# A transformer layer on one core: query norm in two portions, modulation pieces re-timed, a scaling moved to VectorE

## The chip, the cores and the metric

The kernel runs on one core of a Trainium2 chip. The metric is the device time of one execution in microseconds (us). The kernel before takes 1704.09 us, the median of three runs (1702.79, 1704.09 and 1705.93 us).

The engines have the names of the profile: PE (TensorE, the matmuls), PEld (its weight loads), DVE (VectorE), ACT (ScalarE), POOL (GpSimd) and SP (SyncE, which here issues DMAs; its queue is SPq). Each engine works through its own queue in order.

## The reference

One layer of a diffusion backbone: 256 latent tokens `x` and 256 context tokens `ctx`, width 2048, everything in fp32. Cut to what matters:

```python
m_lat = adaln(c, w_ada, b_ada)      # silu(c) @ w_ada, six chunks: shift, scale, gate, shift2, scale2, gate2
m_ctx = adaln(c_ctx, w_ada, b_ada)
hc = modulate(rms_norm(ctx, norm1_g), m_ctx[0], m_ctx[1])
ka_c, va_c, kb_c, vb_c = split_kv(hc @ w_in[:, :KV_WIDTH], ...)      # keys are normalised
h = modulate(rms_norm(x, norm1_g), m_lat[0], m_lat[1])
ka, va, kb, vb = split_kv(...); qa, qb, ga, gb = split_qg(h @ w_in, ...)   # q = rms_norm(q)
qa, ka, qb, kb = apply_rope(...)
o_a = gqa(qa, [ka_c, ka], [va_c, va])            # 16 heads, 4 key heads
o_b = diff_attn(qb, [kb_c, kb], [vb_c, vb])      # 8 heads, two softmaxes, then rms_norm of o
merged = sigmoid(ga) * (o_a @ w_br_a) + sigmoid(gb) * (o_b @ w_br_b)
x = x + gate * (merged @ w_out)
x = x + gate2 * swiglu(modulate(rms_norm(x, norm2_g), shift2, scale2))
```

## The kernel before

**Products in three matmuls.** Each weight is split into a high and a low part in the matmul's type, and each product is three matmuls (`mm3`, L241 hi by hi, L242 hi by lo, L243 lo by hi). A weight tile is 128 x 1024 fp32, 512 KB: 256 rows of a group of 512 columns. `load_w` (L221) fetches it on SP's queue (L224) into the ring `wraw` of seven slots, ACT casts it to `whi` (L235), and DVE forms the difference `wlo` (L237). Both rings, `whi` and `wlo`, have three slots, so ACT and DVE can be no more than three weight tiles ahead of PE. With the two query tiles of 128 tokens a weight tile gives 12 matmuls of 128 x 512; in the key and value stage, with four token tiles, 24.

**Stages.** Start; keys and values, in steps of input rows (`kv_group`, two, four and eight and more k-tiles); query groups of 512 columns, gates and attention units side by side (`filler`, `project`, `front`, `back`: 16 units of branch b, then 16 of a); branch A's projection (loop ahead of L989); out-projection (L1075); norm; FFN.

**Modulation.** The shift and scale of the first norm come in pieces of 512 KB (`ada_cond`, L281 to L335) that PE multiplies by the conditioning vectors (L314). They are loaded either into a slot of the `wraw` ring (L294), into a large tile (L299), or, for the pieces n = 2 and 3 of a step of four k-tiles, in two halves into scratch buffers `nr` and `p` (L303). `modulated` makes the high and low input rows `xT` and `cT` from them (L356 to L360). The other modulation vectors (gate chunk 2, scale chunk 4, shift chunk 3, and gate2 in the FFN) are made by DVE: `ada_pieces` (L447) fetches a piece of 512 KB into the `wraw` ring and adds it, times one number of the conditioning vector, onto a row `ada` (L459), placed behind the newest `wlo`. `ada_later` gives out these pieces, and `take(later, n)` takes n of them. `side_work` (L868) takes one every second turn while queries of branch a are not all there, and two in three turns afterwards. What is left is taken in branch A's loop and by `drain(later)` (L989), and `ada_everywhere` (L990) then spreads the shift row over the partitions.

**Query norm and rotation.** `norm_rope` (L481) squares a tile of 128 x 512 on ACT (L490), reduces it on DVE (L492), makes the reciprocal root (`rstd_of`: DVE L123, then POOL's pow L124) and rotates: two products with the tables (L501, L503), a subtraction and an addition over halves (L505, L506), and the product with the reciprocal root (L507). `q_evac` (L743) calls it at once for the first token tile of a query group and, by `after(2)`, two pieces of the weight loop later for the second. `after(n, f)` runs f n pieces later. In a unit of branch b, `back` (L803) copies the output `on` to SBUF, makes its reciprocal root (`rstdo`) and scales `on` by it on ACT (L842).

**Order.** The Tile framework orders each engine's queue by its own scheduler. `tc.issue_after(ins)` puts an instruction behind another one in the queue.

Of the kernel before, what the change touches and what calls it, by code (L numbers as in the profile page):

```python
# [17 lines left out]
P = 128  # L18
# [28 lines left out]
def hybrid_block(ctx: ExitStack, tc: tile.TileContext, t: dict, out: bass.AP):  # L47
# [161 lines left out]
        nc.vector.tensor_scalar(out=neglam, in0=neglam, scalar1=-LAM_INIT, scalar2=None, op0=ALU.add)  # L209


    last_hi, last_lo = [], []

    def load_raw(r0, c0, n=2):
        raw = wp.tile([P, WK, CG], F32, tag="wraw", bufs=WRAW, name="wraw")
# [5 lines left out]

    def load_w(src, r0, c0, nk=WK, in_big=False):
        raw = wp.tile([P, WK, CG], F32, tag="wraw", bufs=WRAW, name="wraw")
        nc.sync.dma_start(out=raw[:, 0:nk], in_=src[r0:r0 + nk * P, c0:c0 + CG].rearrange("(k p) c -> p k c", p=P))  # L224
# [55 lines left out]
    def ada_cond(k0, nk):  # L280
# [4 lines left out]
        for part in range(2):  # L285
            aps = s_ps("ada")
            held = []
            for q in range(0, NKT, kk):
                piece = t["ada_t"][n0].rearrange("p (k c) -> p k c", c=ncol)
                n0 += 1  # L290
                n = q // kk
                if nk < 4 or n > 3:
                    wt = wp.tile([P, 2 * CG], F32, tag="wraw", bufs=WRAW, name="wada").rearrange("p (k c) -> p k c", c=ncol)
                    nc.sync.dma_start(out=wt, in_=piece)  # L294
                elif n < 2:
                    if n == 0:
                        two = big_tile("wada2").rearrange("p (n k c) -> p n k c", n=2, c=ncol)
                    wt = two[:, n]
                    nc.sync.dma_start(out=wt, in_=piece)  # L299
                else:  # L300
                    wt = [scratch("wada1", tag=tag, bufs=b) for tag, b in (("nr", 2), ("p", 4))]
                    for j in range(2):
                        nc.sync.dma_start(out=wt[j], in_=piece[:, j, :])  # L303
                held += [(q + j, wt[j] if nk == 4 and 1 < n < 4 else wt[:, j, :]) for j in range(kk)]
                last = q + kk == NKT
                if k0 and not last:
                    if nk == 4 and n == 3:
                        yield None
                    continue
                for k, rhs in held[::-1] if k0 else held:  # L310
                    g = k % 4
                    early, late_k = k < 4, k >= NKT - 4
                    with tc.issue_after(last_pe[0].ins) if k0 == 1 and k == held[-1][0] else nullcontext():
                        last_pe[0] = nc.tensor.matmul(aps[32 * g:32 * g + 32, 0:ncol], lhsT=cst[:, k, :], rhs=rhs,  # L314
                                                      start=late_k if k0 else early, stop=early if k0 else late_k)
# [168 lines left out]
    def norm_rope(src, br, qk, tok):  # L484
# [14 lines left out]
        else:  # L499
# [5 lines left out]
            nc.vector.tensor_tensor(out=o3[:, :, 0:half], in0=o3[:, :, 0:half], in1=b3[:, :, half:hd], op=ALU.subtract)  # L505
            nc.vector.tensor_tensor(out=o3[:, :, half:hd], in0=o3[:, :, half:hd], in1=b3[:, :, 0:half], op=ALU.add)  # L506
        nc.vector.tensor_tensor(out=o3, in0=o3, in1=r.unsqueeze(2).to_broadcast([P, nh, hd]), op=ALU.mult)  # L507
        return o


# [232 lines left out]
    def q_evac(qT, br):  # L743
# [58 lines left out]
    def back(br, u, pr):  # L802
# [39 lines left out]
        nc.scalar.mul(out=on, in_=on, mul=r)  # L842
# [101 lines left out]
    for cg in range(4):  # L944
# [35 lines left out]
        for k, _ in enumerate(project(w_bra, oT, AH, cg * CG, gated)):  # L980
# [201 lines left out]
```

## Time and profile before

| | before |
|---|---|
| median of three runs | 1704.09 us |
| the profiled execution's own time | 1703.83 us |
| its span, first to last instruction | 1701.7 us |
| PE busy, instructions | 1676.8 us (99%), 7889 |
| DVE busy | 1138.4 us (67%) |
| ACT busy | 779.0 us (46%) |
| mean DMA rate | 243 GB/s |
| mean granted PE clock | 0.997 |

Rows of the profile read so. A timeline row has the start in us, the duration in us, the engine, line, operation, output <- input, shapes, how many; and, in brackets, how long the engine was idle before it and what ended that. Matmuls overlap: at the full clock they start 0.23 us apart and each lasts 0.39. DVE rows overlap slightly too, so prices are taken start to start where rows follow one another. A row of windows has the stretch, its length, the busy time of PE, PEld, DVE, ACT and POOL with the number of instructions, the granted PE clock (1.00 is full), the busy share of the DMA engines and GB/s. A row of waits has the waiting engine and its line, what ended the wait, the sum in us, the number, and the longest.

### The profile page before, as it was taken

To read this page: it belongs to the slowest core of one execution; us is meant where nothing else is said; L and a number is where in the kernel's file an instruction comes from. 1 tells how busy PE (TensorE), PEld (TensorE's weight loads), DVE (VectorE), ACT (ScalarE), POOL (GpSimd) and SP (SyncE) were. 2 spreads that over 40 slices of the span, in tenths; PEclk is the share of its full clock that TensorE was granted. 3 is DMA by queue.
4 is the path that set the end of the run, shared out by engine and by line. 5 is a ranking of instruction groups with operands and counts; after the bars stand their busy time and mean duration, and the time that the engine had idled before them with its cause. 6 is when DMAs were issued, how large, how long until landed. Compare 5 with 4: busy or idle time off the path is not lost.

```text
span 1701.7 us, 21519 instructions
## 1 busy us (share of the span) xinstructions
PE 1676.8 (99%) x7889; PEld 1355.1 (80%) x7889; DVE 1138.4 (67%) x1438; ACT 779.0 (46%) x1071; POOL 209.3 (12%) x296
## 2 busy tenths in 40 slices
PE   7999999999999999999999999999999999999998
PEld 5677778887887778888888888888888888888887
DVE  5665779798687878996666755566666666554454
ACT  5221222246666656577544534444444444333332
POOL 0200002011231210011111101111111111100000
PEclk9999999999999999999999999999999999999999
DMA  9787875778766768776777857788888888766662
GB/s 352 288 316 275 304 253 157 234 252 256 246 180 216 222 225 272 246 238 212 256 265 237 294 175 221 235 263 267 263 272 263 269 274 253 238 218 195 216 207 88
DMA packets 181860, 413.08 MB, mean 243 GB/s; under 512 B 15065, under 2 KB 16298, under 8 KB 181498
## 3 DMA queue, kind: packets, MB, share of 16 engines
q1 hardware_dynamic: 169482, 374.17, 67.3%
q0 software_dynamic: 12272, 37.53, 7.4%
q8 instruction: 62, 1.02, 0.3%
q14 instruction: 44, 0.36, 0.1%
HBM read 395.35 MB, written 16.29 MB: 242 GB/s over the span
## 4 chain that ended last, share of the span: by engine, by line
PE 75%; issue 10%; DVE 6%; DMA 4%; POOL 3%; ACT 2%; SPq 0%; POOLq 0%; DVEq 0%; ACTq 0%
PE mm L241 22%; PE mm L242 22%; PE mm L243 22%; DVE wlo L237 2%; PE ada L314 1%; POOL fturn L1091 1%; ACT whi L235 1%; PE ptp L814 1%; DMA turn_d<-fpart 1%; DMA fturn<-turn_d 1%; DMA wraw<-in_w_in_dram 1%; DVE ada L459 1%; PE mm L401 1%; PE o L835 1%; DVE mx L736 1%
## 5 line engine op out<-in xcount | busy, mean ns | idle before, releaser
L237 DVE TENSOR_TENSOR wlo<-wraw,whi 128x1024 fp32r<-128x1024 f32 x498 | 606.8, 1220 | 443.9 <-ACT whi L235 442.9
L235 ACT CAST whi<-wraw 128x1024 fp32r<-128x1024 f32 x498 | 522.4, 1050 | 714.0 <-PE mm L243 607.2
L242 PE MATMUL mm<-wlo,hT 128*128 128x512 f32 x684 | 266.3, 389 | 0.1
L243 PE MATMUL mm<-whi,hT 128*128 128x512 f32 x684 | 266.1, 389 | 0.0
L241 PE MATMUL mm<-whi,hT 128*128 128x512 f32 x684 | 266.1, 389 | 0.0
L241 PE MATMUL mm<-whi,xT 128*128 128x512 f32 x630 | 252.7, 402 | 1.3 <-ACT xT L359 1.2
L242 PE MATMUL mm<-wlo,xT 128*128 128x512 f32 x630 | 247.0, 392 | 4.3 <-DVE wlo L237 4.3
L243 PE MATMUL mm<-whi,xT 128*128 128x512 f32 x630 | 246.9, 392 | 0.0
L459 DVE SCALAR_TENSOR_TENSOR ada<-wada,vt,ada 128x1024 f32<-128x1024 f32 x120 | 152.0, 1277 | 0.0
L242 PEld LDWEIGHTS mm<-wlo,hT 128*128 128x128 f32 x684 | 128.4, 188 | 27.7 <-DVE wlo L237 0.9
L241 PEld LDWEIGHTS mm<-whi,hT 128*128 128x128 f32 x684 | 128.4, 188 | 26.7
L243 PEld LDWEIGHTS mm<-whi,hT 128*128 128x128 f32 x684 | 128.4, 188 | 26.5
L241 PEld LDWEIGHTS mm<-whi,xT 128*128 128x128 f32 x630 | 118.6, 188 | 32.7 <-issue 7.0
L242 PEld LDWEIGHTS mm<-wlo,xT 128*128 128x128 f32 x630 | 118.8, 189 | 28.2 <-DVE wlo L237 5.7
L243 PEld LDWEIGHTS mm<-whi,xT 128*128 128x128 f32 x630 | 118.5, 188 | 26.0 <-DVE xT L360 0.3
L241 PE MATMUL mm<-whi,fT 128*128 128x512 f32 x354 | 137.5, 388 | 0.5 <-DVE y L1127 0.5
L242 PE MATMUL mm<-wlo,fT 128*128 128x512 f32 x354 | 137.3, 388 | 0.0
L243 PE MATMUL mm<-whi,fT 128*128 128x512 f32 x354 | 137.3, 388 | 0.0
L241 PEld LDWEIGHTS mm<-whi,fT 128*128 128x128 f32 x354 | 66.4, 188 | 15.0 <-issue 0.8
L243 PEld LDWEIGHTS mm<-whi,fT 128*128 128x128 f32 x354 | 66.5, 188 | 13.8
L242 PEld LDWEIGHTS mm<-wlo,fT 128*128 128x128 f32 x354 | 66.4, 188 | 13.7
L241 PE MATMUL mm<-whi,oT 128*128 128x512 f32 x192 | 75.9, 396 | 0.0
(236 smaller groups left out, 2150.4 us busy)
## 6 DMA issues: line engine op xcount, KB each, us to landing
wraw<-in_w_in_dram SPq DMA_DIRECT2D x159, 512.0 KB, 4.7
wada<-in_w_ada_dram SPq DMA_DIRECT2D x128, 512.0 KB, 4.6
wraw<-in_w_ff_gate_dram SPq DMA_DIRECT2D x88, 512.0 KB, 4.6
wraw<-in_w_ff_up_dram SPq DMA_DIRECT2D x88, 512.0 KB, 5.4
wraw<-in_w_ff_down_dram SPq DMA_DIRECT2D x88, 512.0 KB, 4.8
wada<-in_ada_t_dram SPq DMA_DIRECT2D x52, 512.0 KB, 7.8
wraw<-in_w_br_a_dram SPq DMA_DIRECT2D x32, 512.0 KB, 5.3
wraw<-in_w_out_dram SPq DMA_DIRECT2D x32, 512.0 KB, 5.2
```

Of the source, the lines that this page charges most:

```text
L235: last_hi.append(nc.scalar.copy(out=hi[:, 0:nk], in_=raw[:, 0:nk]))
L237: last_lo.append(nc.vector.tensor_tensor(out=lo[:, 0:nk], in0=raw[:, 0:nk], in1=hi[:, 0:nk].bitcast(F32), op=ALU.subtract))
L241: nc.tensor.matmul(ps, lhsT=ah, rhs=wh, start=first, stop=False, skip_group_check=skip)
L242: nc.tensor.matmul(ps, lhsT=ah, rhs=wl, start=False, stop=False, skip_group_check=skip)
L243: return nc.tensor.matmul(ps, lhsT=al, rhs=wh, start=False, stop=last, skip_group_check=skip)
L314: last_pe[0] = nc.tensor.matmul(aps[32 * g:32 * g + 32, 0:ncol], lhsT=cst[:, k, :], rhs=rhs, start=late_k if k0 else early, stop=early if ...
L401: last_pe[0] = nc.tensor.matmul(ps[cg], lhsT=x, rhs=ws0[cg][y], start=(n == 0), stop=(n == 2))
L459: nc.vector.scalar_tensor_tensor(out=dst, in0=wt, scalar=sc[:, 0, kt:kt + 1], in1=dst, op0=ALU.mult, op1=ALU.add)
L736: nc.vector.tensor_reduce(out=mx, in_=sp, axis=AX.X, op=ALU.max, negate=True)
L814: nc.tensor.transpose(out=tp[:, kt * P:(kt + 1) * P], in_=p[:, kt * P:(kt + 1) * P], identity=ident)
L835: nc.tensor.matmul(op[:, 0:BV], lhsT=pT[:, kt, :], rhs=vb[:, kt, hh * BV:(hh + 1) * BV], start=(kt == 0), stop=(kt == 3))
L1091: nc.gpsimd.dma_start(out=whole[32 * b:32 * b + 32].rearrange("p (k a j) -> p k a j", k=4, a=4), in_=blocks[b])
```

## The change

1. **Modulation pieces at the start.** In `ada_cond`, the pieces of the step k0 = 4 all go into the `wraw` ring, and are multiplied in two batches of eight k instead of one of sixteen. For the steps k0 = 8 and 12 the loads are placed behind the newest weight load, and the pieces that used `nr` and `p` use `nr` twice and `sq` with `pTb`.
2. **Query norm in two portions.** The last three DVE operations of `norm_rope` for queries are put behind the newest `wlo`, one piece later. The second token tile's norm comes three pieces later, not two.
3. **The scaling of `on`** moves from ACT to DVE.
4. **Modulation pieces later.** `side_work` takes one piece in three turns. `drain(later)` and the spreading of the shift row move from ahead of the out-projection to its third column group, and each weight piece of the first two column groups takes one modulation piece.

```diff
-                if nk < 4 or n > 3:
-                    wt = wp.tile([P, 2 * CG], F32, tag="wraw", bufs=WRAW, name="wada").rearrange("p (k c) -> p k c", c=ncol)
-                    nc.sync.dma_start(out=wt, in_=piece)
...
-                    wt = [scratch("wada1", tag=tag, bufs=b) for tag, b in (("nr", 2), ("p", 4))]
...
+                with tc.issue_after(last_load[-1].ins) if k0 >= 8 else nullcontext():
+                    if k0 < 8 or n > 3:
...
+                        wt = [scratch("wada1", tag=tag, bufs=2) for tag in (("nr", "nr") if n == 2 else ("sq", "pTb"))]
...
-                if k0 and not last:
-                    if nk == 4 and n == 3:
+                if k0 and not last and (k0 != 4 or n != 3):
+                    if k0 >= 8 and n == 3:
...
-        nc.vector.tensor_tensor(out=o3, in0=o3, in1=r.unsqueeze(2).to_broadcast([P, nh, hd]), op=ALU.mult)
+        def rest():
+            if tok is not None:
+                nc.vector.tensor_tensor(out=o3[:, :, 0:half], in0=o3[:, :, 0:half], in1=b3[:, :, half:hd], op=ALU.subtract)
+                nc.vector.tensor_tensor(out=o3[:, :, half:hd], in0=o3[:, :, half:hd], in1=b3[:, :, 0:half], op=ALU.add)
+            nc.vector.tensor_tensor(out=o3, in0=o3, in1=r.unsqueeze(2).to_broadcast([P, nh, hd]), op=ALU.mult)
+        if qk == "k":
+            rest()
+        else:
+            def behind():
+                with tc.issue_after(last_lo[-1].ins):
+                    rest()
+            after(1, behind)
...
-                after(2, lambda: norm(tk, ps))
+                after(3, lambda: norm(tk, ps))
...
-        nc.scalar.mul(out=on, in_=on, mul=r)
+        nc.vector.tensor_scalar(out=on, in0=on, scalar1=r, scalar2=None, op0=ALU.mult)
...
-            take(later, 1 if turns[0] % (3 if a_done else 2) else 0)
+            take(later, 1 if turns[0] % 3 == 0 else 0)
...
-    drain(later)
-    b_all = ada_everywhere("b_all", 2)
...
+        if cg == 2:
+            drain(later)
+            b_all = ada_everywhere("b_all", 2)
+        for _ in project(w_out, mT, NKT, cg * CG, out_evac(cg), **(dict(tail=TURN2, hook=tail_hook, in_big=(6, 7)) if cg == 3 else {})):
+            take(later, 1)
```

How the instructions move, at three places. SP's queue in the key and value stage, before; `wada` are modulation pieces (those with 512 elements are the halves for scratch buffers), `wraw` weight tiles, `tok_t` token tiles:

```order
L179 DMA cs<-in_rope_dram 128x384
L224 DMA wraw<-in_w_in_dram 128x2x512
L303 DMA wada_737<-in_ada_t_dram 128x512
L303 DMA wada_738<-in_ada_t_dram 128x512
L303 DMA wada_741<-in_ada_t_dram 128x512
L303 DMA wada_742<-in_ada_t_dram 128x512
L224 DMA wraw<-in_w_in_dram 128x2x512
L294 DMA wada<-in_ada_t_dram 128x1024
L303 DMA wada_860<-in_ada_t_dram 128x512
L294 DMA wada<-in_ada_t_dram 128x1024 x3
L224 DMA wraw<-in_w_in_dram 128x2x512
```

The same place after:

```order
L179 DMA cs<-in_rope_dram 128x384
L224 DMA wraw<-in_w_in_dram 128x2x512
L295 DMA wada<-in_ada_t_dram 128x1024 x4
L224 DMA wraw<-in_w_in_dram 128x2x512
L295 DMA wada<-in_ada_t_dram 128x1024
L170 DMA tok_t_686<-in_x_t_dram 128x1024
L170 DMA tok_t_686<-in_ctx_t_dram 128x1024
L295 DMA wada<-in_ada_t_dram 128x1024 x3
L224 DMA wraw<-in_w_in_dram 128x2x512
```

No half piece is left here, so nothing in SP's queue waits for a scratch buffer; the two token tiles, which stood behind the last of these weight tiles before, now stand ahead of it.

DVE's queue in the query group that runs beside branch b's units (the group whose `nr` reads `rp_qa`), from one `wlo` towards the next, before:

```order
L237 TENSOR_TENSOR wlo<-wraw,whi 128x1024
L123 TENSOR_SCALAR rstdo<-sso 128x1
L459 SCALAR_TENSOR_TENSOR ada_2770<-wada_5070,vt,ada_2770 128x1024
L492 TENSOR_REDUCE ss<-sq 128x4
L501 TENSOR_TENSOR nr<-mm,rp_qa 128x512
L123 TENSOR_SCALAR rstd<-ss 128x4
L503 TENSOR_TENSOR sq<-mm,rp_qa 128x512
L736 TENSOR_REDUCE mx<-s 128x1
L505 TENSOR_TENSOR nr<-nr,sq 128x4x64
L506 TENSOR_TENSOR nr<-nr,sq 128x4x64
L736 TENSOR_REDUCE mx<-s 128x1
L507 TENSOR_TENSOR nr<-nr,rstd 128x512
```

The same place after, between the same two weight tiles:

```order
L237 TENSOR_TENSOR wlo<-wraw,whi 128x1024
L123 TENSOR_SCALAR rstdo<-sso 128x1
L853 TENSOR_SCALAR on<-on,rstdo 128x128
L493 TENSOR_REDUCE ss<-sq 128x4
L502 TENSOR_TENSOR nr<-mm,rp_qa 128x512
L123 TENSOR_SCALAR rstd<-ss 128x4
L504 TENSOR_TENSOR sq<-mm,rp_qa 128x512
L747 TENSOR_REDUCE mx<-s 128x1
L508 TENSOR_TENSOR nr<-nr,sq 128x4x64
L509 TENSOR_TENSOR nr<-nr,sq 128x4x64
L747 TENSOR_REDUCE mx<-s 128x1
L510 TENSOR_TENSOR nr<-nr,rstd 128x512
```

The `ada` is gone from between the two, and the scaling of `on` has come in, directly behind its `rstdo`. The three last operations of the norm (L508 to L510) have not moved: no `wlo` stands ahead of them here.

DVE's queue in the next query group, at the norm of its second token tile, before:

```order
L501 TENSOR_TENSOR nr<-mm,rp_qa 128x512
L123 TENSOR_SCALAR rstd<-ss 128x4
L503 TENSOR_TENSOR sq<-mm,rp_qa 128x512
L459 SCALAR_TENSOR_TENSOR ada_5370<-wada_5706,vt,ada_5370 128x1024
L505 TENSOR_TENSOR nr<-nr,sq 128x4x64
L506 TENSOR_TENSOR nr<-nr,sq 128x4x64
L237 TENSOR_TENSOR wlo<-wraw,whi 128x1024
L507 TENSOR_TENSOR nr<-nr,rstd 128x512
```

The same place after:

```order
L502 TENSOR_TENSOR nr<-mm,rp_qa 128x512
L123 TENSOR_SCALAR rstd<-ss 128x4
L504 TENSOR_TENSOR sq<-mm,rp_qa 128x512
L237 TENSOR_TENSOR wlo<-wraw,whi 128x1024
L508 TENSOR_TENSOR nr<-nr,sq 128x4x64
L509 TENSOR_TENSOR nr<-nr,sq 128x4x64
L460 SCALAR_TENSOR_TENSOR ada_2800<-wada_5570,vt,ada_2800 128x1024
L510 TENSOR_TENSOR nr<-nr,rstd 128x512
```

Here the `wlo` now stands ahead of the `ada` and of the two rotation operations.

Later in SP's queue, branch A's 32 weight tiles and the out-projection's 32 stood one behind the other before, with no modulation piece between them. Now 16 pieces stand among branch A's tiles (four in each column group, one behind each of its last four tiles), and 13 among the first 13 tiles of the out-projection, so that 17 tiles in a row have one piece each.

More of the change, by code (lines that the diff above doesn't have):

```diff
@@ L209, in lambdas @@
         nc.vector.tensor_scalar(out=neglam, in0=neglam, scalar1=-LAM_INIT, scalar2=None, op0=ALU.add)
-    last_hi, last_lo = [], []
+    last_hi, last_lo, last_load = [], [], []
     def load_raw(r0, c0, n=2):
@@ L223, in load_w @@
         raw = wp.tile([P, WK, CG], F32, tag="wraw", bufs=WRAW, name="wraw")
-        nc.sync.dma_start(out=raw[:, 0:nk], in_=src[r0:r0 + nk * P, c0:c0 + CG].rearrange("(k p) c -> p k c", p=P))
+        last_load.append(nc.sync.dma_start(out=raw[:, 0:nk], in_=src[r0:r0 + nk * P, c0:c0 + CG].rearrange("(k p) c -> p k c", p=P)))
         return split_w(raw, nk, in_big)
@@ L291, in ada_cond @@
                 n = q // kk
-                if nk < 4 or n > 3:
-                    wt = wp.tile([P, 2 * CG], F32, tag="wraw", bufs=WRAW, name="wada").rearrange("p (k c) -> p k c", c=ncol)
-                    nc.sync.dma_start(out=wt, in_=piece)
[L295 to L300, printed above, removed]
-                    wt = [scratch("wada1", tag=tag, bufs=b) for tag, b in (("nr", 2), ("p", 4))]
-                    for j in range(2):
-                        nc.sync.dma_start(out=wt[j], in_=piece[:, j, :])
@@ L304, in ada_cond @@
-                held += [(q + j, wt[j] if nk == 4 and 1 < n < 4 else wt[:, j, :]) for j in range(kk)]
+                with tc.issue_after(last_load[-1].ins) if k0 >= 8 else nullcontext():
+                    if k0 < 8 or n > 3:
+                        wt = wp.tile([P, 2 * CG], F32, tag="wraw", bufs=WRAW, name="wada").rearrange("p (k c) -> p k c", c=ncol)
+                        nc.sync.dma_start(out=wt, in_=piece)
+                    elif n < 2:
+                        if n == 0:
+                            two = big_tile("wada2").rearrange("p (n k c) -> p n k c", n=2, c=ncol)
+                        wt = two[:, n]
+                        nc.sync.dma_start(out=wt, in_=piece)
+                    else:
+                        wt = [scratch("wada1", tag=tag, bufs=2) for tag in (("nr", "nr") if n == 2 else ("sq", "pTb"))]
+                        for j in range(2):
+                            nc.sync.dma_start(out=wt[j], in_=piece[:, j, :])
@@ L305, in ada_cond @@
+                held += [(q + j, wt[j] if k0 >= 8 and 1 < n < 4 else wt[:, j, :]) for j in range(kk)]
                 last = q + kk == NKT
-                if k0 and not last:
-                    if nk == 4 and n == 3:
+                if k0 and not last and (k0 != 4 or n != 3):
+                    if k0 >= 8 and n == 3:
                         yield None
                     continue
+                first_ks, last_ks = (range(0, 4), range(12, 16)) if k0 == 0 else (range(4, 8), range(8, 12)) if k0 == 4 else (range(12, 16), range(0, 4))
@@ L310, in ada_cond @@
                 for k, rhs in held[::-1] if k0 else held:
                     g = k % 4
-                    early, late_k = k < 4, k >= NKT - 4
                     with tc.issue_after(last_pe[0].ins) if k0 == 1 and k == held[-1][0] else nullcontext():
                         last_pe[0] = nc.tensor.matmul(aps[32 * g:32 * g + 32, 0:ncol], lhsT=cst[:, k, :], rhs=rhs,
-                                                      start=late_k if k0 else early, stop=early if k0 else late_k)
+                                                      start=k in first_ks, stop=k in last_ks)
@@ L503, in norm_rope @@
             nc.vector.tensor_tensor(out=b3, in0=s3, in1=tb[:, tok, 1, :].unsqueeze(1).to_broadcast([P, nh, hd]), op=ALU.mult)
-            nc.vector.tensor_tensor(out=o3[:, :, 0:half], in0=o3[:, :, 0:half], in1=b3[:, :, half:hd], op=ALU.subtract)
-            nc.vector.tensor_tensor(out=o3[:, :, half:hd], in0=o3[:, :, half:hd], in1=b3[:, :, 0:half], op=ALU.add)
-        nc.vector.tensor_tensor(out=o3, in0=o3, in1=r.unsqueeze(2).to_broadcast([P, nh, hd]), op=ALU.mult)
+        def rest():
[5 more added lines that the diff above has]
+            rest()
+        else:
+            def behind():
+                with tc.issue_after(last_lo[-1].ins):
+                    rest()
+            after(1, behind)
         return o
@@ L1074, in hybrid_block @@
     for cg in range(4):
-        drain(project(w_out, mT, NKT, cg * CG, out_evac(cg), **(dict(tail=TURN2, hook=tail_hook, in_big=(6, 7)) if cg == 3 else {})))
+        if cg == 2:
[3 more added lines that the diff above has]
+            take(later, 1)
     NFT = DFF // P
```

## The prediction

> **What bounds the kernel now.** First the page's line of engines, then the waits of PE, then the stretches in which they lie.
>
> ```profile
> PE 1676.8 (99%) x7889; PEld 1355.1 (80%) x7889; DVE 1138.4 (67%) x1438; ACT 779.0 (46%) x1071; POOL 209.3 (12%) x296
> ```
>
> PE is busy for 99% of the span, and the change takes no matmul away. So it can only win idle time of PE, or time in which PE ran below its full clock.
>
> ```profile
> PE mm L242 <- DVE wlo L237: 4.3, 2, 3.0
> PE mm L241 <- DVE kb L442: 2.7, 1, 2.7
> PE mm L241 <- ACT xT L359: 1.2, 1, 1.2
> ```
>
> ```profile
> 50.00:75.00 25.00, 21.13 (x116) 15.93 (x115) 19.80 (x38) 5.34 (x8) 10.02 (x32) 0.98 0.75 284
> 75.00:100.00 25.00, 25.00 (x139) 15.99 (x138) 12.93 (x18) 5.36 (x6) 0.00 (x0) 0.95 0.83 296
> 550.00:575.00 25.00, 22.02 (x115) 17.29 (x113) 20.53 (x37) 17.08 (x36) 4.94 (x4) 1.00 0.63 202
> 575.00:600.00 25.00, 25.00 (x118) 19.04 (x119) 21.49 (x30) 12.47 (x25) 5.21 (x3) 0.93 0.84 272
> 625.00:650.00 25.00, 23.71 (x115) 19.49 (x114) 24.78 (x39) 14.86 (x25) 2.03 (x2) 1.00 0.70 225
> 893.00:941.00 48.00, 48.00 (x213) 39.77 (x212) 28.07 (x31) 21.67 (x26) 6.54 (x12) 1.00 0.75 244
> ```
>
> These are the stages that the change touches. Three of them have idle PE: 3.87 us in 50 to 75 (stall A), 2.98 in 550 to 575 (B), 1.29 in 625 to 650 (C). After A and B the granted clock falls: 25 x (0.02 + 0.05) = 1.75 us at A, 25 x 0.07 = 1.75 at B. After C it does not. That makes 11.6 us in all. The out-projection (893 to 941) has no idle PE.
>
> **Part 1, the start (A).** The stall's chain, from the timeline of all engines:
>
> ```profile
> 61.81 0.33 SPq L303 DMA_DIRECT2D wada<-in_ada_t_dram  x1
> 63.68 0.57 SPq L224 DMA_DIRECT2D wraw<-in_w_in_dram  x1
> 70.83 1.04 ACT L235 CAST whi<-wraw 128x1024 fp32r<-128x1024 f32 x1 [5.84 <-DMA wraw<-in_w_in_dram]
> 73.79 0.50 PE L241 MATMUL mm<-whi,cT 128*128 128x512 f32 x1 [2.65 <-DVE kb L442]
> 75.33 0.63 PE L242 MATMUL mm<-wlo,cT 128*128 128x512 f32 x1
> ```
>
> ```profile
> SPq L303 <- POOL rp_kb L198: 10.1, 1, 10.1
> ```
>
> SP stood 10.1 us before a half piece (L303) whose scratch buffer POOL still used, and the weight tile behind it in the queue could not be asked for until 63.68. Its cast began at 70.83, when it had come; on DVE the evacuations (L442) that free PE's accumulators stand behind its `wlo`, and PE waited 2.65 us for them, and then ran slow (0.63 us for a matmul). After the change no scratch piece is left here, so the 10.1 us go, and the DMA engines, which were busy for only 0.75 of the stretch, start sooner. What comes late next is the transfer itself: from the first of the four pieces to the second weight tile stand 12 transfers of 512 KB (10 pieces and tiles, two token tiles). The rates for them:
>
> ```profile
> 110.00:115.00 5.00, 5.00 (x24) 4.01 (x23) 5.00 (x11) 1.94 (x6) 0.00 (x0) 1.00 1.04 406
> 640.00:645.00 5.00, 5.00 (x30) 4.24 (x29) 5.00 (x9) 4.12 (x9) 0.00 (x0) 1.00 0.94 312
> ```
>
> 0.524 MB takes 1.29 us at 406 GB/s and 1.68 at 312. SP had issued all before the blocked half by 51.5, so 12 transfers end between 51.5 + 15.5 = 67.0 and 51.5 + 20.2 = 71.7, where the tile was there at 70.8 before. PE needs it 2.65 us earlier, at 68.2. The stall that is left is so between 0 and the whole; I take 0.6, near the fast end, because this stretch carries the same large transfers as the one with 406. The wait of 1.22 for `xT` stays: its modulation chain is not shortened, and the first batches of four k now stand behind it. The loss of clock goes with the long wait (1.22 drew none). Gain 2.65 - 0.6 + 1.75 = **3.8** (0 to 4.4).
>
> **Part 2 and 3, the query group beside branch b (B).** DVE, ACT, POOL and PE there:
>
> ```profile
> 566.09 1.28 DVE L459 SCALAR_TENSOR_TENSOR ada<-wada,vt,ada 128x1024 f32<-128x1024 f32 x1
> 567.28 0.68 DVE L492 TENSOR_REDUCE ss<-sq 128x4 f32<-128x512 f32 x1
> 567.81 0.40 ACT L842 ACTIVATE on<-on,rstdo 128x128 f32<-128x128 f32 x1 [1.87 <-POOL rstdo L124]
> 573.67 1.21 DVE L237 TENSOR_TENSOR wlo<-wraw,whi 128x1024 fp32r<-128x1024 f32 x1
> 574.93 0.50 PE L242 MATMUL mm<-wlo,xT 128*128 128x512 f32 x1 [2.98 <-DVE wlo L237]
> ```
>
> ```profile
> 556.37 0.40 ACT L842 ACTIVATE on<-on,rstdo 128x128 f32<-128x128 f32 x1 [2.36 <-POOL rstdo L124]
> 565.36 0.58 ACT L490 ACTIVATE sq<-mm 128x512 f32<-128x512 f32 x1
> ```
>
> The block from `ss` to the `wlo` takes 573.67 - 567.28 = 6.39 us on DVE. The split into portions does not shorten it, since no weight tile comes to stand in it. It is the block's start that moves. Before, ACT waited 2.36 and 1.87 us for POOL's pow with the next `whi` casts queued behind, DVE waited for those casts, and an `ada` of 1.19 us stood ahead of `ss`. After, ACT waits for nothing there, the preceding `whi` and `wlo` come up to 2.4 us earlier, and the `ada` goes in while DVE would idle. Then `ss` waits for its input alone: the squares that ACT took at 565.36, of a product whose last matmul began at 563.36 and was done 0.6 us later. Squares from 564.0 to 564.6, the block from 564.6 to 571.0, its `wlo` to 572.2, where PE wants it at 574.93 - 2.98 = 571.95. I take a stall of 0.3 (0 to 0.9, if `on` holds DVE for one pow). At 0.3 no clock is lost. Gain 2.98 - 0.3 + 1.75 = **4.4** (2.1 to 4.7).
>
> The new wait is that of `on` on DVE for POOL: 16 of them, with `ss`, `wlo` and everything else behind.
>
> ```profile
> ACT on L842 <- POOL rstdo L124: 33.0, 16, 4.0
> L124 POOL TENSOR_TENSOR rstdo<-rstdo,neghalf x16: 548/1456/3204, 395.4 to 614.6; 128x1 f32<-128x1 f32 x16
> 544.32 0.57 POOL L124 TENSOR_TENSOR rstdo<-rstdo,neghalf 128x1 f32<-128x1 f32 x1
> 566.32 1.46 POOL L124 TENSOR_TENSOR rstdo<-rstdo,neghalf 128x1 f32<-128x1 f32 x1 [9.99 <-DVE rstdo L123]
> 400.00:440.00 40.00, 30.05 (x45) 1.00 0.78 243
> ```
>
> The pow took 0.55 to 3.2 us (median 1.46): 0.57 with no long DVE operation beside it, 1.46 beside the `ada` of 566.09. A DVE that waits for it runs nothing beside it, so 0.57 is nearer. A unit is (614.6 - 395.4) / 15 = 14.6 us; between query groups DVE idles 40 - 30.05 = 10 us in 40 (400 to 440), 3.6 a unit, and that hides the pow and `on` (about 0.25, less than ACT's 0.40) at either price. Nothing in the sum. [...]
>
> **The next group (C), and an earlier one.**
>
> ```profile
> 633.45 1.27 DVE L459 SCALAR_TENSOR_TENSOR ada<-wada,vt,ada 128x1024 f32<-128x1024 f32 x1
> 635.31 1.22 DVE L237 TENSOR_TENSOR wlo<-wraw,whi 128x1024 fp32r<-128x1024 f32 x1
> 636.58 0.50 PE L242 MATMUL mm<-wlo,xT 128*128 128x512 f32 x1 [1.29 <-DVE wlo L237]
> ```
>
> The `wlo` passes the `ada` and two rotations, 635.31 - 633.45 = 1.86 us, more than the 1.29 that PE waited: gain **1.3** (0.6 to 1.3). In branch b's own second group an `ada` comes ahead of the `wlo` that ends the block:
>
> ```profile
> 374.93 1.22 DVE L237 TENSOR_TENSOR wlo<-wraw,whi 128x1024 fp32r<-128x1024 f32 x1
> 376.99 0.40 PE L242 MATMUL mm<-wlo,xT 128*128 128x512 f32 x1
> ```
>
> The `wlo` was done at about 376.15, 0.84 before its matmul; 1.2 later leaves a wait of 0.4. Loss **0.5** (0 to 1.2).
>
> **Part 4, the pieces.** The fewer pieces in `side_work` only empty DVE and the DMA queue there. Where they go, at 17 tiles in a row with one each, two things get full.
>
> ```profile
> 897.23 1.22 DVE L237 TENSOR_TENSOR wlo<-wraw,whi 128x1024 fp32r<-128x1024 f32 x1 [1.50 <-ACT whi L235]
> 899.95 1.22 DVE L237 TENSOR_TENSOR wlo<-wraw,whi 128x1024 fp32r<-128x1024 f32 x1 [1.50 <-ACT whi L235]
> 906.53 1.28 DVE L1010 TENSOR_TENSOR y<-mm,a 128x512 f32<-128x512 f32 x2
> wraw<-in_w_out_dram SPq DMA_DIRECT2D x32, 512.0 KB, 5.2
> ```
>
> A tile is 2.72 us, of which DVE idles 1.50; an `ada` of 1.19 fits. Per column group that leaves 8 x 0.3 = 2.5 us against six evacuations of 0.6 = 3.6: about 1 us short, which the two tiles that DVE is ahead cover. The DMAs: 17 x 2 x 0.524 = 17.8 MB, and 52 GB/s of other traffic (244, less 192 for a tile in 2.72 us), 2.4 MB in the 46.2 us that PE takes: 20.2 MB, or 438 GB/s. At 406 GB/s it takes 49.8 us, at 312 64.8; at the stretch's own 244 / 0.75 = 325, 62.2. The seven slots cover 7 x 2.72 less the landing of 5.2 and the `wlo` of 1.2, 12.6 us. Late beyond that: 0, 6.0 and 3.4 us. I take a loss of **1.5** (0 to 6), between the fast row and the stretch's own. [...]
>
> **The sum.** -3.8 - 4.4 - 1.3 + 0.5 + 1.5 = -7.5 us, against the profiled execution of 1703.83: 1696.3. That execution lies 0.26 under the median of 1704.09, which takes the same shift: 1696.6.
>
> **The rivals.**
> (1) *Block B keeps its place*, because something other than ACT's wait holds its start: then the split does nothing there, -4.4 goes, and the sum is -3.1: **1701.0**. For it: the order shows the same nine operations between the two weight tiles. Against it: the waits of 2.36 and 1.87 on ACT. 13%.
> (2) *The start is bound by DMA*: the 12 transfers at 312 GB/s end at 71.7, and A stays, clock and all: -3.7, **1700.4**. For it: 284 GB/s in the stretch; against it: 0.75 busy. 11%.
> (3) *The pieces fill the out-projection's DMA*: at 312, a loss of 6.0 in place of 1.5: -3.0, **1701.1**. 10%.
> (4) *Slower: DVE waits for POOL's queue.* POOL also issues the stores of the gates, each waiting for ACT's evacuation:
>
> ```profile
> POOL gate_d L859 <- ACT gate L858: 29.6, 7, 6.7
> ```
>
> If a pow stands behind such a store, DVE now waits for all of it: 4.2 on average, the issue and the pow 0.55 each, `on` 0.25, 5.6 us. DVE's 3.6 of idle hide the rest, and 2.0 x 7 = 14 come through: +6.5, **1710.6**. It decides from a wait of 3.6 us on. Against it: ACT, which stood at the same place before, never waited longer than 4.0, and 2.1 on average. 6%.
> (5) *The lost clock is not the stalls' doing.* Then 3.5 us do not come back: -4.0, **1700.1**. For it: C's wait of 1.29 drew no loss, and two cases are few. Against it: the clock falls right behind both long waits (0.95 and 0.93) and in no other of the quoted stretches. 5%. [...]
>
> **How the numbers follow.** No change is taken as within 0.2%, 3.4 us, which is about what a measurement of this kernel can tell. The forecast has 55%. All good ends of its terms together give -10.4, 1693.7, and I go 1.2 below that, for small waits of PE that DVE with fewer pieces may end too; the bad ends do not come together, and two of the worst (A or B by half, and the out-projection at 325 GB/s) give some 1700. Rivals 1, 2, 3 and 5 lie at the border, 1700.1 to 1701.1, and half of their 39% counts as faster. So faster 0.76, the same 0.18, slower 0.06. With the rivals the range is 1692.5 to 1701.5.
>
> **What would show it.** Right: no wait of SP for POOL in 50 to 64; PE idle under 2 us in the stretch of A, of which 1.2 for `xT`; the clock 1.00 in the stretches behind A and B; the wait for `wlo` at B under 1 us; `on` on DVE behind a pow of about 0.6. Wrong: a wait for `wlo` of more than 2 us at B; `whi` waiting for DMA between 880 and 945; DVE waits for `rstdo` that add up to more than 30 us.

## The result and the profile after

The changed kernel takes 1696.71 us, the median of six runs (1694.54 to 1698.39), beside 1703.44 for the kernel before in the same comparison (six runs, 1700.08 to 1705.93). The ratio is 0.9962, with a 95% interval of 0.9949 to 0.9975: faster by 0.25% to 0.51%. The profiled execution has a span of 1694.2 us, 7.5 less than before. By the medians the gain is 6.7 us. Forecast were 1696.6 us and a sum of -7.5.

The page's line of engines and the waits of PE, after:

```profile
PE 1675.4 (99%) x7889; PEld 1352.9 (80%) x7889; DVE 1144.5 (68%) x1454; ACT 776.8 (46%) x1055; POOL 195.1 (12%) x296
...
PE mm L242 <- DVE wlo L237: 1.8, 3, 1.1
...
PE o L846 <- DVE qT L247: 1.2, 1, 1.2
...
PE mm L241 <- ACT cT L360: 0.3, 1, 0.3
```

The three waits that bounded the kernel are gone: 2.7 for `kb`, 3.0 and 1.3 for `wlo`. Two new ones have come: 1.2 for `qT`, and 1.8 for `wlo` at other places, 1.6 of it in the out-projection. The stretches show where:

```profile
50.00:75.00 25.00, 24.07 (x135) 16.74 (x134) 19.48 (x37) 5.00 (x8) 8.96 (x32) 1.00 0.79 297
75.00:100.00 25.00, 24.79 (x134) 16.08 (x133) 14.56 (x21) 5.59 (x8) 0.00 (x0) 1.00 0.90 330
550.00:575.00 25.00, 25.00 (x129) 19.97 (x128) 22.24 (x42) 15.28 (x32) 3.51 (x4) 1.00 0.52 165
575.00:600.00 25.00, 23.81 (x114) 19.47 (x113) 16.79 (x22) 15.63 (x26) 1.70 (x3) 1.00 0.77 247
625.00:650.00 25.00, 25.00 (x120) 20.80 (x119) 17.64 (x22) 13.64 (x20) 1.14 (x2) 1.00 0.79 253
...
893.00:941.00 48.00, 46.22 (x203) 36.23 (x203) 35.32 (x37) 20.48 (x26) 7.67 (x14) 1.00 1.01 364
```

The granted clock is 1.00 in all of them, and PE idles 1.78 us in the out-projection, where it idled for none.

A sum over the whole is had from the starts of the same five matmuls in both traces:

| matmul | before | after | difference so far | in the stretch |
|---|---|---|---|---|
| last on context rows (end of keys and values) | 324.15 | 320.02 | -4.13 | -4.13 |
| first of branch B's projection | 687.29 | 676.11 | -11.18 | -7.05 |
| first of the out-projection | 884.13 | 872.57 | -11.56 | -0.38 |
| first FFN product from a ring tile | 978.96 | 971.82 | -7.14 | +4.42 |
| the last | 1697.43 | 1690.17 | -7.26 | -0.12 |

Branch B's projection (`o_b @ w_br_b`) runs beside the last attention units, so the third stretch holds these units and the projections of both branches. One group of modulation matmuls (`adac`, 8 matmuls, 1.0 us) left the second stretch for the third, and another the third for the fourth. So the queries and attention up to there gain 6.05 and the out-projection loses 3.4. This ledger is read for every experiment below.

### The profile page after: what moved, and what is told of

Same layout as the page of the kernel before. It is cut to its first block, busy times and chain, and to the rows that moved or that the text cites. A ratio compares the mean times of both kernels' runs of the same rounds, so it can differ in the third digit from the quotient of the medians.

```text
span 1694.2 us, 21504 instructions
## 1 busy us (share of the span) xinstructions
PE 1675.4 (99%) x7889; PEld 1352.9 (80%) x7889; DVE 1144.5 (68%) x1454; ACT 776.8 (46%) x1055; POOL 195.1 (12%) x296
## 4 chain that ended last, share of the span: by engine, by line
PE 91%; DMA 3%; DVE 3%; issue 1%; ACT 1%; POOL 0%; SPq 0%; DVEq 0%; ACTq 0%; POOLq 0%
PE mm L241 27%; PE mm L242 27%; PE mm L243 27%; DMA wraw<-in_w_out_dram 2%; PE ada L315 2%; PE ptp L825 1%; DVE wlo L237 1%; DMA wraw<-in_w_in_dram 1%; PE o L846 1%; PE mm L402 1%; PE s L801 1%; ACT whi L235 1%; DMA wraw<-in_w_ff_gate_dram 0%; PE s L241 0%; PE o L241 0%
```

## The experiments

Each was timed beside the kernel before; ratios are against it. "Stretch" is a column of the ledger, as the difference from before. Each ratio is known to some 0.12%, so two of them tell the difference between two changed kernels only to about 3 us; what is smaller is read from the ledger.

**1. ScalarE keeps the scaling.** The change without its part 3:

```diff
-        nc.vector.tensor_scalar(out=on, in0=on, scalar1=r, scalar2=None, op0=ALU.mult)
+        nc.scalar.mul(out=on, in_=on, mul=r)
```

> The change with part 3 undone: the scaling of `on` back on ScalarE, everything else as changed. Theory 1 (as in the prediction: ScalarE's wait for GpSimd's pow, with the weight casts queued behind it, is what held the block at stall B back): the wait for `wlo` at B comes back with 1.5 to 3 us, with a dip of the clock behind it: 2 to 4.5 us slower than the changed kernel, about 1699 to 1701. Theory 2 (the modulation piece that no longer stands in the block and beside the pow is what freed it): ScalarE waits under 1 us for each pow, no wait over 0.5 us at B, within 1 us of the changed kernel.

Measured: 1697.81 us, ratio 0.9969 (0.9958 to 0.9981), 1.1 us above the changed kernel. PE's wait at B, from the timeline, and what ACT waited for:

```profile
569.29 0.50 PE L242 MATMUL mm<-wlo,xT 128*128 128x512 f32 x1 [1.01 <-DVE wlo L237]
...
ACT on L853 <- POOL rstdo L124: 24.5, 15, 3.9
```

Neither theory holds alone. A wait comes back, but 1.0 us of 3.0 and with no dip of the clock behind it. The queries' stretch is -4.41, against -7.05 with `on` on DVE. So with fewer pieces the block's start is held less, and ACT's wait still holds it somewhat.

**2. The norm in one portion.** The change without its part 2:

```diff
-        if qk == "k":
-            rest()
-        else:
-            def behind():
-                with tc.issue_after(last_lo[-1].ins):
-                    rest()
-            after(1, behind)
+        rest()
...
-                after(3, lambda: norm(tk, ps))
+                after(2, lambda: norm(tk, ps))
```

> The change with part 2 undone: the query norm in one portion, the second token tile two pieces later, everything else as changed. Theory (the split moves nothing at B, only at C): no wait over 0.5 us at B; at C a wait for `wlo` of 0 to 1.3 us; 0 to 1.5 us slower than the changed kernel. Rival (the split is what ends the wait at B): a wait of 2 us or more there and the clock dip with it, 4 us slower.

Measured: 1694.55 us, ratio 0.9951 (0.9938 to 0.9965): not slower, where 0 to 1.5 us slower was expected. All the waits of PE between 550 and 650 are one row:

```profile
PE o L840 <- DVE qT L247: 1.2, 1, 1.2
```

No wait at B and none at C, and a queries' stretch of -7.36 against -7.05. The split, from which the change has its name, does nothing here, as the order had shown for B; at C too, where the theory had left it up to 1.3. Without the other parts it was not tried.

**3. The modulation pieces in scratch buffers again.** The change with the `ada_cond` of before:

```diff
-                    if k0 < 8 or n > 3:
+                if nk < 4 or n > 3:
...
-                        wt = [scratch("wada1", tag=tag, bufs=2) for tag in (("nr", "nr") if n == 2 else ("sq", "pTb"))]
+                    wt = [scratch("wada1", tag=tag, bufs=b) for tag, b in (("nr", 2), ("p", 4))]
```

> The change with part 1 undone: the first norm's modulation pieces loaded and multiplied as before. Theory (stall A is SyncE's wait for a scratch buffer that GpSimd holds): the wait of 2.7 us near 74 and the clock dip behind it come back, 3 to 4.4 us slower than the changed kernel, PE idle 3.5 to 4 us in 50 to 75. Rival (the start is bound by the DMA rate, the stall had only moved): within 1 us of the changed kernel.

Measured: 1698.48 us, ratio 0.9974 (0.9963 to 0.9984), 1.8 us above the changed kernel, between the two theories. Stall A is back, with its clock:

```profile
PE mm L241 <- DVE kb L442: 2.0, 1, 2.0
...
75.00:100.00 25.00, 25.00 (x139) 15.59 (x138) 12.72 (x18) 5.36 (x6) 0.00 (x0) 0.95 0.85 300
```

The first stretch is -1.83 against -4.13: 2.3 us of the 3 to 4.4. Single traces of this stretch scatter: the nine kernels of this study that have part 1 show -3.29 to -5.34, 4.40 on average, the three without it (before among them) 0 to -1.83, 0.77 on average. Part 1 is so worth some 3.6 us, and a single pair of traces tells it only to about one.

**4. The pieces early.** The change without its part 4:

```diff
-            take(later, 1 if turns[0] % 3 == 0 else 0)
+            take(later, 1 if turns[0] % (3 if a_done else 2) else 0)
...
             take(gates, 1 if cg else (0, 0, 0, 0, 2, 2, 3, 0)[k])
+    drain(later)
+    b_all = ada_everywhere("b_all", 2)
...
-        if cg == 2:
-            drain(later)
-            b_all = ada_everywhere("b_all", 2)
```

> The change with part 4 undone: the modulation pieces at the old rate in the side work and the rest ahead of the out-projection, everything else as changed. At the out-projection no wait of PE is left (it had 3.3 us of lost time in the changed kernel): 3.3 us faster there. At B, theory 1 (ScalarE's wait held the block): no wait over 0.9 us in spite of the piece that stands in the block again, so the whole is about 2.5 to 3.3 us faster than the changed kernel, about 1693.5 to 1694.5. Theory 2 (the piece held it): the wait at B comes back with 1.5 to 3 us and a clock dip of up to 1.75, so the whole is within 1.5 us of the changed kernel, either way.

Measured: 1693.82 us, ratio 0.9947 (0.9934 to 0.9959), 2.9 us below the changed kernel by the medians, as theory 1 had it. The ledger has less: 1.0 us over the three stretches that part 4 touches. The block at B with its piece again, on DVE; and PE's only wait for `wlo` between 550 and 650, at C:

```profile
558.70 1.27 DVE L460 SCALAR_TENSOR_TENSOR ada<-wada,vt,ada 128x1024 f32<-128x1024 f32 x1
559.89 0.68 DVE L493 TENSOR_REDUCE ss<-sq 128x4 f32<-128x512 f32 x1
...
566.46 1.22 DVE L237 TENSOR_TENSOR wlo<-wraw,whi 128x1024 fp32r<-128x1024 f32 x1
...
627.63 0.50 PE L242 MATMUL mm<-wlo,xT 128*128 128x512 f32 x1 [1.04 <-DVE wlo L237]
```

The piece stands ahead of the block again, directly before `ss`, and there is no wait at B. At C the wait is back, although the split has put the two rotations behind the `wlo`. So part 4 is what ends C, and it costs more in the out-projection (+4.42, of which 1.0 is the moved group of matmuls, against +0.76 here) than it gains.

**5. The scaling alone.** The kernel before with part 3 and nothing else:

```diff
-        nc.scalar.mul(out=on, in_=on, mul=r)
+        nc.vector.tensor_scalar(out=on, in0=on, scalar1=r, scalar2=None, op0=ALU.mult)
```

> The kernel before with part 3 alone: the scaling of `on` on VectorE, nothing else changed. VectorE's block at stall B has the same operations as before, its modulation piece among them, and 0.2 us of `on` more. Theory 1 (ScalarE's wait with the weight casts behind it held the block): the wait of 3.0 us at B falls under 1 us and the clock dip of 1.75 us goes: 3.5 to 4.7 us faster than before. Theory 2 (the piece in the block held it): the wait stays at 2 us or more, within 1 us of before.

Measured: 1697.55 us, ratio 0.9967 (0.9955 to 0.9979): 5.6 us from one line (3.6 to 7.7 by the interval), 4.4 of it in the queries' stretch. Before, the cast of the weight tile ahead of the block, and the matmul that PE had reached then:

```profile
563.82 1.04 ACT L235 CAST whi<-wraw 128x1024 fp32r<-128x1024 f32 x1
...
564.99 0.47 PE L241 MATMUL mm<-whi,xT 128*128 128x512 f32 x1
```

Here, the same tile on ACT and DVE, the block's start, the same matmul, and PE's first wait behind it:

```profile
559.38 1.04 ACT L235 CAST whi<-wraw 128x1024 fp32r<-128x1024 f32 x1
...
560.45 1.23 DVE L237 TENSOR_TENSOR wlo<-wraw,whi 128x1024 fp32r<-128x1024 f32 x1 [0.44 <-ACT whi L235]
...
562.84 0.68 DVE L492 TENSOR_REDUCE ss<-sq 128x4 f32<-128x512 f32 x1
...
563.51 0.47 PE L241 MATMUL mm<-whi,xT 128*128 128x512 f32 x1
...
575.75 0.51 PE L242 MATMUL mm<-wlo,xT 128*128 128x512 f32 x1 [0.56 <-DVE wlo L237]
```

That matmul starts at 563.51 against 564.99, 1.48 earlier. The cast starts at 559.38 against 563.82, and `ss` at 562.84 against 567.28: both 4.44 earlier, 2.96 of it against PE. That is the 2.98 that PE had waited, with the same operations in the block and the scaling besides. The 0.56 is for a later tile, whose `wlo` stands behind an `on` that waited 0.45 for POOL. Theory 1 is shown: it is ACT's wait, with the casts behind it, that set the block's start.

The four combinations at B are then: neither part, 2.98 us and a dip; the scaling alone, no wait before the block's tile and 0.56 later; fewer pieces without the scaling (experiment 1, which has parts 1 and 2 too), 1.01; both, none. Two remedies overlap, and either would have taken away the dip.

**6 and 7. What is full in the out-projection.** Two kernels that leave part of the computation out: in the first the out-projection's pieces aren't loaded, and VectorE does the same work on the row itself; in the second they are loaded, and VectorE adds 8 of 1024 columns.

```diff
+            if in_out:
+                wt = dst
+            else:
+                wt = wp.tile([P, 1024], F32, tag="wraw", bufs=WRAW, name="wada2")
+                nc.sync.dma_start(out=wt, in_=w_ada[kt * P:(kt + 1) * P, chunk * D + hf * 1024: chunk * D + (hf + 1) * 1024])
```

```diff
+            w_use = 8 if in_out else 1024
...
-                    nc.vector.scalar_tensor_tensor(out=dst, in0=wt, scalar=sc[:, 0, kt:kt + 1], in1=dst, op0=ALU.mult, op1=ALU.add)
+                    nc.vector.scalar_tensor_tensor(out=dst[:, 0:w_use], in0=wt[:, 0:w_use], scalar=sc[:, 0, kt:kt + 1], in1=dst[:, 0:w_use], op0=ALU.mult, op1=ALU.add)
```

> The changed kernel, but the out-projection's modulation pieces aren't loaded: VectorE does the same operation on the row itself (part of the computation is left out: the shift row gets wrong summands). Theory (DMA is full there): PE's waits in the out-projection, 3.3 us of lost time in the changed kernel, go to under 0.7, and ScalarE's casts wait for no DMA there. Rival (VectorE is full there, 1 us short in each column group): at least 2 us of them stay.

> The changed kernel, but of the out-projection's modulation pieces VectorE adds only 8 of 1024 columns (the rest of these sums is left out); they are loaded as before. Theory (DMA is full there): at least 2 us of the 3.3 us of lost PE time stay. Rival (VectorE is full there): under 0.7 us is left.

Measured: 1693.64 us without the loads (ratio 0.9949, 0.9936 to 0.9963) and 1696.30 without the sums (0.9959, 0.9944 to 0.9974). The stretch 885 to 933 without the loads:

```profile
885.00:933.00 48.00, 48.00 (x216) 38.80 (x216) 37.51 (x39) 20.61 (x25) 7.70 (x14) 1.00 0.83 274
```

The same stretch without the sums, and what ACT's casts waited for there:

```profile
885.00:933.00 48.00, 46.66 (x204) 36.20 (x203) 28.84 (x38) 20.45 (x25) 7.67 (x14) 1.00 1.00 364
...
ACT whi L235 <- DMA wraw<-in_w_out_dram: 19.6, 10, 5.4
```

With VectorE's work kept (37.51 us of 48) and the loads gone, PE has no idle time; with VectorE's work cut to 28.84 and the loads kept, PE still idles 1.34 us. The ledger says the same: the out-projection's stretch is +1.14 without the loads and +5.54 without the sums, against +4.42, and 1.0 of each is the moved group of matmuls. It is the loads, as expected; VectorE's shortage is covered. What the two kernels can't separate is the rate of the DMAs from the ring: a piece that isn't loaded takes no slot of `wraw` either.

**8. The pieces where the DMAs have room.** The changed kernel with two pieces in three turns from the second unit of branch a on, so that 13 pieces are left for branch A's projection and none for the out-projection:

```diff
-            take(later, 1 if turns[0] % 3 == 0 else 0)
+            take(later, 1 if (turns[0] % 3 if a_units else turns[0] % 3 == 0) else 0)
...
+    a_units = []
...
+        if n == 17:
+            a_units.append(True)
```

> The changed kernel with one number moved: one piece in three turns only until the second unit of branch a, two in three from there, so that 13 pieces stand among branch A's tiles and none among the out-projection's. Theory (17 tiles with a piece each overfill the DMAs): the out-projection's loss of 3.3 us goes, B and C stay without a wait, the wait of 1.2 us for `qT` near 578 stays: 2.5 to 3.3 us faster than the changed kernel, about 1693.5 to 1694, span about 1691. Rival (the pieces cost the same wherever they are): within 1 us of the changed kernel, with new waits between 600 and 800.

Measured: 1693.10 us, ratio 0.9943 (0.9931 to 0.9956), span 1691.2, as the theory had it: 3.0 below the changed kernel's span. The out-projection's stretch of the ledger is -0.14 instead of +4.42; the third stretch, with both projections, is +1.78 instead of -0.38. Part of the agreement is scatter: 1.2 of the 3.0 lie in the first stretch (-5.34 against -4.13) and 0.6 in the last, where the edit changes nothing, and 1.2 in the three that it touches. PE's waits between 550 and 650 are the 1.2 us for `qT` alone.

**9 and 10. One portion, and `qT` earlier.** Part 2 undone on top of experiment 8; and then also the transposition of the query tile one piece earlier:

```diff
-            after(5, turn)
+            after(4, turn)
```

> The kernel with pieces two in three from branch a's second unit, and part 2 undone as well (norm in one portion). Theory (the split does nothing where the waits were): within 1 us of the former kernel, 1692 to 1694, no wait for `wlo` at B or C above 0.5 us. Rival (the split saves time that the rate of the pieces hid): 1.5 us or more slower, with such a wait.

> As the kernel of one portion and later pieces, and the query tile's transposition four pieces behind its norm instead of five, which puts the first `qT` ahead of the score's maximum and two weight tiles on VectorE. Theory (the wait of 1.2 us near 577 is for the accumulator that this `qT` frees late): the wait goes, 1 to 1.2 us faster than the kernel of one portion and later pieces. Rival (the accumulator is held by another reader as late): the wait stays over 0.8 us, no difference beyond 0.5 us.

Measured: 1693.31 us (0.9949, 0.9936 to 0.9963) and 1693.53 (0.9951, 0.9938 to 0.9963). The first agrees that the split does nothing: PE's only wait between 550 and 650 is again the 1.2 for `qT`. The second misses: the wait for `qT` is gone, but PE waits at the same line for the next reader of such an accumulator, and the time is the same.

```profile
PE o L840 <- ACT o L851: 0.7, 1, 0.7
```

The best kernels (pieces early, in the middle, and in the middle in one portion) are 0.51% to 0.57% faster than before; their intervals overlap one another and that of the changed kernel. No one of them is shown to be the best.

## Why the prediction was right, point by point

**The whole.** -7.5 was forecast against the profiled execution; the ledger has -7.26, the spans -7.5 and the medians -6.7. That the sum came so close is luck in part. The out-projection lost 1.9 more than forecast (3.4 for 1.5); against it stand 0.3 more at the start, 0.85 more in the queries (6.05 for 5.2), and 0.5 in the third and the last stretch, where nothing was forecast. The mechanism at B was the right one. At A, at C and for the pow the size was right and the reason was not.

**The start, 3.8.** The size held: the stretch shows 4.13, and part 1's own share is about 3.6. SP waits for POOL no more, as forecast. But the weight tile behind which the stall stood, the tenth, does not come earlier. Its cast began at 70.83 before; now it begins at 74.19. The ninth, cast at 57.08 before, is late too:

```profile
65.23 1.05 ACT L235 CAST whi<-wraw 128x1024 fp32r<-128x1024 f32 x1 [2.32 <-DMA wraw<-in_w_in_dram]
...
69.02 0.38 SPq L224 DMA_DIRECT2D wraw<-in_w_in_dram  x1
...
74.19 1.06 ACT L235 CAST whi<-wraw 128x1024 fp32r<-128x1024 f32 x1 [7.50 <-DMA wraw<-in_w_in_dram]
```

The step that failed is the start of the transfers. The working let SP issue all twelve by 51.5. The pieces now need slots of the ring, and SP waits for them, between 40 and 75 us, 11.6 us until PE's modulation matmuls free slots and 5.3 until the ninth `wlo` frees one. So the tenth tile is asked for at 69.02 only:

```profile
SPq L295 <- PE ada L315: 11.6, 6, 7.9
SPq L224 <- DVE wlo L237: 5.3, 1, 5.3
```

By the prediction's own rule (PE needs the tile at 68.2) the whole stall should have stayed. It went because the order on DVE changed. Before, the tenth `wlo` stood ahead of the evacuations that PE waited for:

```profile
71.90 1.23 DVE L237 TENSOR_TENSOR wlo<-wraw,whi 128x1024 fp32r<-128x1024 f32 x1 [5.20 <-ACT whi L235]
73.05 2.48 DVE L442 TENSOR_TENSOR kb<-mm,kb 128x512 f32<-128x512 f32 x4
```

After, it stands behind all of them:

```profile
75.89 0.69 DVE L443 TENSOR_TENSOR kb<-mm,kb 128x512 f32<-128x512 f32 x1 [0.67 <-PE mm L243]
76.50 1.22 DVE L237 TENSOR_TENSOR wlo<-wraw,whi 128x1024 fp32r<-128x1024 f32 x1
```

With part 1 undone (experiment 3) the old order is back, with a `wlo` at 70.97, five evacuations from 72.11 and the wait. So the gain belongs to part 1, and that its size was forecast is luck. Which of part 1's edits makes the new order, and how much the modulation matmuls add that PE now does in smaller groups between, no run separates. The wait of 1.22 for `xT`, which was to stay, is gone too; in its place are 0.6 for a modulation piece and 0.3 for `cT`.

**B, 4.4.** Right, and shown by experiments 4 and 5. The block after:

```profile
558.32 0.29 DVE L853 TENSOR_SCALAR on<-on,rstdo 128x128 f32<-128x128 f32 x1 [0.66 <-POOL rstdo L124]
558.52 0.68 DVE L493 TENSOR_REDUCE ss<-sq 128x4 f32<-128x512 f32 x1
...
564.90 1.22 DVE L237 TENSOR_TENSOR wlo<-wraw,whi 128x1024 fp32r<-128x1024 f32 x1
```

It is 564.90 - 558.52 = 6.38 us long, 6.39 before: the split shortened nothing, as said. It started 567.28 - 558.52 = 8.76 us earlier, 5.04 of which PE itself had gained by then (the matmul that stood at 564.99 now stands at 559.95), so 3.7 against PE, where 2.7 were forecast, and no wait is left. Forecast was also that the `ada` taken out of the block matters; experiment 4 shows that it need not have been.

**`on` waiting for POOL, nothing in the sum.** Right in size, wrong in the reason. The rows of the tile `rstdo`, after:

```profile
L124 POOL TENSOR_TENSOR rstdo<-rstdo,neghalf x16: 548/558/1520, 392.2 to 603.2; 128x1 f32<-128x1 f32 x16
...
  POOL rstdo L124: 9.2, 15
```

The pow fell from a median of 1456 ns to 558. The reason given was that a DVE which waits for it runs nothing beside it. The same row with the scaling on ACT (experiment 1), and then with it on DVE but the pieces as before (experiment 5):

```profile
L124 POOL TENSOR_TENSOR rstdo<-rstdo,neghalf x16: 548/559/2682, 392.2 to 605.9; 128x1 f32<-128x1 f32 x16
```

```profile
L124 POOL TENSOR_TENSOR rstdo<-rstdo,neghalf x16: 548/1468/2067, 394.9 to 610.1; 128x1 f32<-128x1 f32 x16
```

So the pow is short (medians of 558 and 559 ns) where part 4 has taken pieces away, whoever waits for it, and long (1456 before, 1468 here) where a piece still stands behind `rstdo` on DVE; with part 4 alone undone (experiment 4) the median is 1462. ACT had waited 33.0 us in all; DVE waits 9.2, 0.6 at a time, in time that it had to spare. Rival 4 is so refuted.

**C, 1.3.** Right in size, wrong in cause: the wait goes because part 4 takes the piece from ahead of the `wlo`, not because the split lets the `wlo` pass. It stays gone with the norm in one portion (experiment 2) and comes back, at 1.04, with the pieces and the split together (experiment 4).

**The earlier group of branch b, +0.5.** Wrong: no wait came. The `wlo` does come late, about as forecast. It starts at 372.04 and lasts 1.22, where PE could have used it from about 372.8. But in the new order another matmul of the high parts and two transpositions stand ahead of the one that needs it, and PE works through these:

```profile
372.04 1.22 DVE L237 TENSOR_TENSOR wlo<-wraw,whi 128x1024 fp32r<-128x1024 f32 x1
...
372.43 0.73 PE L241 MATMUL mm<-whi,xT 128*128 128x512 f32 x2
373.01 0.38 PE L761 MATMUL qtp<-ident,nr 128*128 128x128 f32 x2
373.31 0.50 PE L242 MATMUL mm<-wlo,xT 128*128 128x512 f32 x1
```

I had priced the delay and not looked at what else PE's queue has to do meanwhile.

**The out-projection, +1.5 (0 to 6).** The mechanism was right, the size too small: 3.4. The rate was not the error; it was 364 GB/s at a share of 1.01, better than the 325 that the working leaned on. At 364 the 20.2 MB take 55.5 us, 9.3 more than PE, and the cover of 12.6 us should have hidden that. The cover was the mis-sized term: it counts seven slots of weight tiles when the run begins. With a piece behind each tile half of the slots hold pieces. The loads of the out-projection's 32 tiles, with the first and the last issue, before and after:

```profile
L224 SPq DMA_DIRECT2D wraw<-in_w_out_dram x32: 367/368/368, 861.3 to 947.4; - x32
```

```profile
L224 SPq DMA_DIRECT2D wraw<-in_w_out_dram x32: 367/368/368, 861.5 to 940.6; - x32
```

The first was asked for 22.9 us before PE's first matmul with it (884.13); now it is 11.1 (872.57). The DMAs are at a share of 1.00 from branch A's pieces on (840 to 872), and the out-projection's tiles are late from the start:

```profile
840.00:872.00 32.00, 32.00 (x147) 26.51 (x146) 26.90 (x27) 15.32 (x19) 3.83 (x7) 1.00 1.00 362
```

```profile
883.88 1.06 ACT L235 CAST whi<-wraw 128x1024 fp32r<-128x1024 f32 x1 [2.55 <-DMA wraw<-in_w_out_dram]
```

Such waits of `whi` for the DMAs, which the prediction had named as a sign of being wrong, came: nine from 879 to 945, 15.7 us in all on ACT.

**Not seen at all:** the new wait of 1.2 us for `qT`. PE's next accumulator of that ring is free only when DVE has read the query tile out of it; with other pieces in its queue, DVE does that behind a `wlo` that waits for its `whi`:

```profile
576.56 1.23 DVE L237 TENSOR_TENSOR wlo<-wraw,whi 128x1024 fp32r<-128x1024 f32 x1 [0.58 <-ACT whi L235]
577.70 0.75 DVE L808 SCALAR_TENSOR_TENSOR p<-p,rs 128x512 f32<-128x512 f32 x1
578.36 0.68 DVE L247 TENSOR_TENSOR qT<-qtp,qT 128x512 fp32r<-128x512 f32 x1
```

That the wait disappears with the pieces early, where the `qT` stands ahead of `p`, fits this; that it is only worth 1.2 us where nothing else is as late is what experiment 10 showed.

**Rivals 1, 2, 3 and 5.** 1 is refuted by experiment 5. Of 2 the late transfers came, later than it said (a cast at 74.19, for an end at 71.7), but stall A did not stay: PE idles 0.93 us there and the clock is 1.00. 3 was right in kind and at 3.4 of its 6.0 us. 5 is refuted: where the long wait goes, at A or at B, the clock stays at 1.00, and where it comes back (experiment 3), the clock falls to 0.95.

## What to carry to other kernels

A small operation that waits for another engine (here for POOL's pow, 1.46 us in the median, on which ACT waited 33.0 us in all) should not stand in the queue that feeds the bottleneck: moving one 128 x 128 scaling from ACT, where weight casts stood behind its wait, to DVE brought 5.6 of the kernel's 1703 us by itself, the largest gain of a part in these runs. Remedies for one wait do not add up: with fewer pieces in place, taking the scaling back costs only 1.1 us (2.6 in its stretch). Work that is moved to fill a later stage has to be set against that stage's DMA traffic and against the lead that is left when it begins, not against a full ring. A buffer ring that two kinds of transfers share gives each of them only a part of its lead: here the first tile of the out-projection was asked for 11.1 us ahead, where it was 22.9. And the name of a change is not its effect: beside the other parts the split of the norm did nothing, and the order of the instructions had shown that at the place that counted.

## What was not expected of the hardware

The granted clock of PE fell after idle times between matmuls of 2.02 us (experiment 3), 2.51 (experiment 5, at A), 2.65 and 2.98 (before), and not after 1.85 (experiment 7), 1.62 (experiment 5, at C), 1.29 or 1.22 (before). The record of the clock begins at 12.76 us in the trace of before and at 13.08 in that of after; idle times ahead of that are not counted. The two falls of before are to 0.50 and last 3.41 us each, so each costs 1.7 us; in experiment 5 the clock of 0.83 from 70 to 80 gives 1.7 as well. In experiments 3 and 5 the matmuls behind the idle time start 0.43 us apart for a while, in place of 0.23. With 1.7 us a fall, for experiment 3 an estimate from the others, these idle times cost 1.6 to 1.8 times themselves. The first fall of before:

```profile
74.20:77.61 3.41, 3.41 (x10) 2.64 (x9) 2.02 (x4) 0.00 (x0) 0.00 (x0) 0.50 1.02 408
```

The rows with the longest idle time without a fall (experiment 7) and the shortest with one (experiment 3):

```profile
63.41 1.06 PE L315 MATMUL ada<-wada,cst 128*32 128x512 f32 x8 [1.85 <-DMA wada<-in_ada_t_dram]
```

```profile
72.85 0.50 PE L241 MATMUL mm<-whi,cT 128*128 128x512 f32 x1 [2.02 <-DVE kb L442]
```

The length alone may not decide. At the end of before the clock falls to 0.50 at 1698.94 us, 1.23 us after the end that the trace gives for the last matmul, though 1.29 at C and the 1.85 of experiment 7 drew no fall. In the trace of before the recorded clock changes at 74.20, 77.61, 575.96, 579.37 and 1698.94 us; with the start of the record at 12.76 these lie 18, 1, 146, 1 and 328 times 3.413 us apart. What sets these times is not shown. So few falls are no rule, and of idle times between matmuls none from 1.85 to 2.02 was measured.

Over 48 us with weights and pieces side by side (893 to 941, after) the DMAs moved 364 GB/s at a share of 1.01, above the 325 that the share of 0.75 at 244 in the same stretch before had suggested: the busy share of 0.75 was here no measure of what the DMA engines could move.
